# Hybrid encoder trunk on one core: down units in groups of four, a seventeenth weight tile, expert splits three ahead

## The chip, the cores and the metric

The kernel runs on one core of a Trainium2 chip. The metric is the device time of one execution in microseconds (us). Engines are named as the profile names them: PE (TensorE matmul), PEld (TensorE weight load), ACT (ScalarE), DVE (VectorE), POOL (GpSimd), SP (SyncE, which here issues the weight DMAs; SPq is its queue).

## The reference, cut to what matters

256 tokens of width 1024 go through two layers, all in float32. Layer 0 is a gated short convolution and a dense SwiGLU; layer 1 is differential attention and a mixture of eight experts. The part of this case is the mixture:

```
logits = t @ router                      # 256 tokens, 8 experts
top_v, top_i = top_k(logits, 2)          # two experts each, gates = softmax(top_v)
for e in range(8):
    out += combine[:, e] * ((silu(t @ w1[e]) * (t @ w3[e])) @ w2[e])
# w1[e], w3[e]: 1024 x 3584 ("up"); w2[e]: 3584 x 1024 ("down"); float32
```

The weights of the eight experts are 352.3 MB, and each of them is read once.

## The kernel before

**Units and tiles.** All weights pass through one `Stream` (L104 to L196). Its pieces are units of at most 128 x 2048 float32, which is 1 MB, or 8 KB of each partition. A unit is loaded by one DMA on SP (`load`, L142) into a *tile*, one of `SLOTS` = 16 buffers of 8 KB. The list `free` gives tiles out at its front and takes them back at its end.

**Wide and narrow experts.** The experts are ranked by their number of tokens; ranks 0 to 3 are *wide* (room for 128 tokens), ranks 4 to 7 *narrow* (64 tokens). `ORDER` makes them alternate: wide, narrow, wide, narrow and so on.
- A *wide unit* has to be split before use (`split_to`, L168): ACT writes the rounded upper part `whi` into a second tile (L180), DVE writes the rest `wlo` into a third one (L182), and the raw tile goes back to the list. PE then makes 12 matmuls of 512 columns with it (`proj`, L430): for each of two row blocks first the pass with `whi`, then the one with `wlo`, then again `whi` (two banks each). The two tiles go back once PE is done.
- A *narrow unit* is used as it is loaded (`proj_narrow`, L1138): 8 float32 matmul instructions, no split, one tile. Of the 32 up units of a narrow expert the last 16 are 768 KB (384 columns), all others are 1 MB.

**How far ahead.** After the matmuls of a unit, `release` (L192) gives its tiles back, splits the units up to `SPL` = 4 ahead of the one just used, and calls `fill`, which issues loads as long as there are free tiles and `spare` (L125) allows it. `spare` keeps back only what the splits of the next `AHEAD` = 8 releases need. ACT, DVE and PE each run in the order written. A new use of a tile waits for the end of the old one: a `whi` in a former raw tile waits for the DVE split that read it, a `whi` in a tile of a used unit waits for PE.

**Stages.** The mixture has nine stages (L1248). Stage e does the up units of the e-th expert and the down units of the one before it: 28 up units of a wide expert or 32 of a narrow one, and 14 down units. Stages 1, 3, 5 and 7 have narrow up units and wide down units, stages 2, 4 and 6 wide up and narrow down units; stage 0 has only up units (wide), stage 8 only down units (narrow). `merged` (L251) writes the order inside a stage: from the eighth up unit on, one down unit after each two up units, and what is left at the end.

**What else lies in a stage.** Counted in up units, `stage` (L1157) calls hooks: after the 3rd and the 6th the result of the expert before is scattered back to the tokens (`sct`, L1224 and L1225), after the 17th come the transposes of the route back, after the 22nd the tokens of the next expert are gathered (`tp`, L953 for a wide and L968 for a narrow one; the two parts of L953 lie one unit apart). When a chunk of hidden columns is done, ACT makes the SiLU (L1185), DVE multiplies (L1111, L1125), and four and five units later PE transposes the result (`tp`, L1105), which ACT and DVE then write back (L98, L99, L1130) into the `g3` tiles of 2 KB (`GT` = 16).

Of the kernel before, what the change touches and what calls it, by code (L numbers as in the profile page):

```python
# [36 lines left out]
LAMBDA_INIT = 0.8 - 0.6 * math.exp(-0.3 * 1)  # L37

UNIT = 2048
SLOTS = 16  # L40
SPL = 4
AHEAD = 8
GT = 16
GB = 3
HB = 1
NARROW = 64
# [23 lines left out]
def kernel(ctx: ExitStack, tc: tile.TileContext, x_in, positions, norm_mix, norm_ffn, conv_in,  # L70
                       conv_w, conv_out, attn_in, q_norm, k_norm, lam_q1, lam_k1, lam_q2, lam_k2, subln,
                       attn_out, ffn_w1, ffn_w3, ffn_w2, router, moe_w1, moe_w3, moe_w2, out):
    nc = tc.nc
# [30 lines left out]
    class Stream:  # L104
        def __init__(self, units, whole=0):
            self.units = units
            self.whole = whole
            self.free = list(range(SLOTS))
            self.raw = {}
            self.spl = {}  # L110
            self.nd = 0
            self.ns = 0
            self.done = 0

        def plain(self, i):
            return len(self.units[i]) == 4
# [8 lines left out]
        def spare(self):  # L125

            free, ns = len(self.free) - 1, self.ns
            for done in range(self.done, self.done + AHEAD):
                if free < 0:
                    return False  # L130
                while ns < min(done + SPL, len(self.units)):
                    if not self.plain(ns):
                        free -= 2
                        if free < 0:
                            return False
                        free += 1 if ns < self.nd else 0
                    ns += 1
                if done < len(self.units):
                    free += self.size(done)
            return True  # L140
# [51 lines left out]
        def release(self):  # L192
            self.free += self.spl.pop(self.done)[1]
            self.done += 1
            self.split_to(self.done - 1 + SPL)
            self.fill()  # L196

    def cols(w, c0, cw, k0, nk):
# [39 lines left out]
    WCH = [(0, 1024), (1024, 1024), (2048, 1024), (3072, 512)]  # L238
    NCH = [(0, 2048), (2048, 1536)]
    NDN = DFE * D // (P * UNIT)  # L240
    WAIT = 6

    def up_plan(narrow):

        for c0, cw in NCH if narrow else WCH:
            m = KD if narrow else KD * cw // UNIT
            for which in range(2):
                for j in range(m):
                    yield c0, cw, which, j, m

    def merged(up, down, narrow=False):  # L251

        d = 0
        for c, u in enumerate(up_plan(narrow) if up else ()):
            yield "up", u
            while down and d < (c + 1 - WAIT) // 2:
                yield "down", d
                d += 1
        for i in range(d, NDN if down else 0):
            yield "down", i  # L260

    def stage_units(up, w2, plain_up=False, plain_down=False):

        us = []
        for kind, u in merged(len(up) > 0, w2 is not None, plain_up):
            if kind == "up":
                c0, cw, which, j, m = u
                unit, plain = cols(up[which], c0, cw, j * KD // m, KD // m), plain_up
            else:
                unit, plain = pairs(w2, u), plain_down  # L270
            us.append((*unit, True) if plain else unit)
        return us
# [27 lines left out]
    st = Stream(units, n_static)  # L300
# [143 lines left out]
    def whole(xs, k0=0):  # L444
        return lambda k: (*xs, k0 + k)
# [62 lines left out]
    with ph1:  # L508
# [33 lines left out]
        for j in range(4):  # L542
            pc = cproj(3 * j)
            csb = work.tile([P, 512], F32, name="csb", tag="w0")
            S.activation(csb, pc, AF.Copy)
            spare(2)
            pv = cproj(3 * j + 1)
            u = work.tile([P, 2, NT], F32, name="u", tag="w1")
            V.tensor_tensor(u.rearrange("p m t -> p (m t)"), pv, csb, op=OP.mult)
            cv = work.tile([P, 2, NT], F32, name="cv", tag="w1")  # L550
            for m in range(2):
                wc = [cw_col[:, jj * 8 + 2 * j + m:jj * 8 + 2 * j + m + 1] for jj in range(3)]
                V.tensor_scalar(cv[:, m, :], u[:, m, :], wc[1], None, op0=OP.mult)
                for jj, o, i in ((0, slice(1, NT), slice(0, NT - 1)), (2, slice(0, NT - 1), slice(1, NT))):
                    V.scalar_tensor_tensor(cv[:, m, o], u[:, m, i], wc[jj], cv[:, m, o], op0=OP.mult, op1=OP.add)
            spare(2)
            pb = cproj(3 * j + 2)
            z = work.tile([P, 2, NT], F32, name="z", tag="w0")
            V.tensor_tensor(z, pb.rearrange("p (m t) -> p m t", m=2), cv, op=OP.mult)
            if j % 2 == 0:  # L560
                zt[j // 2] = gtile()
            c = slice(2 * (j % 2), 2 * (j % 2) + 2)
            split(zt[j // 2][0][:, c, :], zt[j // 2][1][:, c, :], z)
            spare(2)
# [76 lines left out]
    with ExitStack() as ph:  # L641
# [158 lines left out]
        down = Down(u0, 4, lambda k0: whole((oh, ol), k0))  # L800
# [97 lines left out]
    def one_hot(e, slots, scale=None, table=None):  # L898

        table = posm if table is None else table  # L900
        pe = p3.tile([P, NB, P], F32, name="pe", tag="pe", bufs=2)
        for b in range(NB):
            if scale:
                late["V"] = V.tensor_scalar(pe[:, b, :], slots, table[:, b, e:e + 1], scale[b], op0=OP.is_equal,
                                            op1=OP.mult)
            else:
                V.tensor_scalar(pe[:, b, :], slots, table[:, b, e:e + 1], None, op0=OP.is_equal)
        return pe
# [199 lines left out]
    def activate(h1, h3, n=0):  # L1108

        g = work.tile([P, 512], F32, name="g", tag="w1")  # L1110
        V.tensor_tensor(g, h3, h1, op=OP.mult)  # L1111
        parts = (p3.tile([P, 4, P], F32R, name="gh3", tag="g3", bufs=GT),
                 p3.tile([P, 4, P], F32R, name="gl3", tag="g3", bufs=GT))

# [7 lines left out]
    def activate_narrow(h1, h3, cw, n=0):  # L1122

        g = work.tile([P, 512], F32, name="g", tag="w1")
        V.tensor_tensor(g[:, :cw], h3, h1, op=OP.mult)  # L1125
        gn = p3.tile([P, 4, P], F32, name="gn3", tag="g3", bufs=GT)

# [29 lines left out]
    def stage(s, u0, xs, gt, hooks=(), bank_of=yd_bank):  # L1157
# [7 lines left out]
        yb = []  # L1165
        c = 0
        for u, (kind, v) in enumerate(merged(xs is not None, gt is not None, narrow), u0):
            if kind == "up":
                c0, cw, which, j, m = v
# [35 lines left out]
    class Back:  # L1205


        def __init__(self, pT, gate, narrow=False, final=False):
            self.pT, self.gate, self.narrow = pT, gate, narrow
            if final:  # L1210
                y = [p3.tile([P, 512], F32R, name=f"y{k}7", tag="g3", bufs=GT) for k in "hl"]
            else:
# [20 lines left out]
                V.tensor_tensor(x[:, b, c], bank, x[:, b, c], op=OP.add)  # L1233

    pe = one_hot(0, slot1, rstds)
    with tc.issue_after(late["S"].ins), tc.issue_after(late["V"].ins):
        st.release()
    xs = gather(pe)
# [8 lines left out]
    with tc.manual_schedule(engines={ET.PE, ET.Activation, ET.DVE}):  # L1247
        for e in range(NE + 1):  # L1248
# [31 lines left out]
            if e == NE:  # L1280
                end = Back(*backs.pop(NE - 1), not is_wide(NE - 1), final=True)
                end.scale(yb)
                for i in range(2):
                    c = slice(i * 512, (i + 1) * 512)
# [188 lines left out]
```

## Time and profile before

| | |
|---|---|
| median of three runs (1304.0, 1308.05, 1308.25) | 1308.05 us |
| profiled execution, its own time | 1304.43 us |
| its span, first to last instruction | 1302.6 us |
| PE busy | 1270.1 us (98%) |
| DVE busy, ACT busy | 754.9 us (58%), 608.6 us (47%) |
| DMA of the weights | 423.33 MB |

The profiled execution ends 1.8 us outside its span, and is 3.6 us shorter than the median. A busy PE is not PE at its peak, so the rows below are read by what a group of matmuls takes from one start to the next. A row of the chain (the work that ended last, followed back from the end) is: start us, duration us, engine, output tile, line, and the number of instructions merged. [...]

### The profile page before, as it was taken

The page shows a single profiled execution, that of the slowest core. Times are in us where ns is not written, and L with a number is a line of the kernel's source. Part 1 is how long each engine was busy: PE and PEld are TensorE (multiplying, and loading weights), DVE is VectorE, ACT ScalarE, POOL GpSimd, SP SyncE. Part 2 cuts the span into 40 slices and gives each one's busy share as a digit, 9 for nine tenths or more (in the row PEclk, how much of TensorE's full clock was granted, in tenths as well). Part 3 has the DMA queues.
Part 4 walks back from the last instruction along what each step waited for, and adds up shares of the span by engine and source line. Part 5 has one row for each costly group of instructions (what it writes and reads, how often), then busy time and mean ns, then how long its engine had stood idle before and what let it go on. Part 6 is the DMA issues. An engine that isn't in the chain of part 4 may idle for free.

```text
span 1302.6 us, 16445 instructions
## 1 busy us (share of the span) xinstructions
PE 1270.1 (98%) x6275; PEld 885.1 (68%) x6275; DVE 754.9 (58%) x995; ACT 608.6 (47%) x674; POOL 2.9 (0%) x12
## 2 busy tenths in 40 slices
PE   6999999999999899999999999999999999999997
PEld 6998888888767788556767546676635676754552
DVE  7976555547776698243865334586524387543340
ACT  5535444436676685234654233565423365523330
POOL 0000000000000000000000000000000000000000
PEclk9999999999999899999999999999999999999998
DMA  7964655546430499999999999999999999999995
GB/s 254 393 207 141 244 176 193 192 129 227 177 130 30 154 345 333 413 425 423 397 423 416 387 426 425 414 399 420 388 425 425 424 393 418 420 389 426 425 426 229
DMA packets 109652, 426.02 MB, mean 327 GB/s; under 512 B 9053, under 2 KB 23422, under 8 KB 87166
## 3 DMA queue, kind: packets, MB, share of 16 engines
q1 hardware_dynamic: 109134, 423.33, 82.6%
q0 software_dynamic: 432, 1.57, 0.3%
q8 instruction: 51, 0.84, 0.2%
q14 instruction: 35, 0.29, 0.1%
HBM read 423.82 MB, written 1.05 MB: 326 GB/s over the span
## 4 chain that ended last, share of the span: by engine, by line
PE 91%; DVE 4%; ACT 2%; DMA 2%; issue 0%; SPq 0%; DVEq 0%; ACTq 0%
PE h L441 33%; PE h L1146 14%; PE y L441 11%; PE y L1146 8%; PE yd L441 8%; PE qkv L441 4%; DVE wlo L182 2%; PE mm L535 2%; PE mm L536 2%; PE mm L534 2%; PE tp L1105 2%; PE tp L953 1%; ACT whi L180 1%; DMA raw<-in_moe_w_dram 1%; PE tp L968 1%; PE tp L421 1%
## 5 line engine op out<-in xcount | busy, mean ns | idle before, releaser
L182 DVE TENSOR_TENSOR wlo<-raw,whi 128x2048 fp32r<-128x2048 f32 (+1 forms) x298 | 536.2, 1823 | 349.9 <-ACT whi L180 302.0
L180 ACT ACTIVATE whi<-raw 128x2048 fp32r<-128x2048 f32 (+1 forms) x298 | 450.9, 1538 | 429.2 <-PE h L441 160.8
L1146 PE MATMUL h<-raw,xn 128*64 128x512 f32 (+1 forms) x1024 | 206.2, 545 | 0.0
L441 PE MATMUL h<-whi,xh 128*128 128x512 f32 x448 | 148.6, 401 | 0.0
L1146 PEld LDWEIGHTS h<-raw,xn 128*64 128x64 f32 x1024 | 68.2, 136 | 117.8 <-issue 111.9
L441 PE MATMUL h<-wlo,xh 128*128 128x512 f32 x448 | 144.3, 392 | 2.3 <-DVE wlo L182 2.3
L441 PE MATMUL h<-whi,xl 128*128 128x512 f32 x448 | 143.7, 390 | 0.0
L1146 PE MATMUL y<-raw,gn 128*64 128x512 f32 x448 | 105.2, 601 | 0.0
L441 PEld LDWEIGHTS h<-whi,xh 128*128 128x128 f32 x448 | 81.2, 189 | 31.5 <-ACT whi L180 9.7
L441 PEld LDWEIGHTS h<-wlo,xh 128*128 128x128 f32 x448 | 83.7, 188 | 21.7 <-DVE wlo L182 4.1
L441 PEld LDWEIGHTS h<-whi,xl 128*128 128x128 f32 x448 | 84.1, 188 | 18.3
L441 PE MATMUL y<-whi,gh 128*128 128x512 f32 x224 | 75.0, 416 | 0.0
L441 PE MATMUL h<-wlo,hh 128*128 128x512 f32 (+1 forms) x192 | 71.9, 375 | 0.0
L441 PE MATMUL h<-whi,hh 128*128 128x512 f32 (+1 forms) x192 | 71.8, 374 | 0.0
L441 PE MATMUL h<-whi,hl 128*128 128x512 f32 (+1 forms) x192 | 71.5, 372 | 0.0
L441 PE MATMUL y<-wlo,gh 128*128 128x512 f32 x224 | 69.4, 391 | 0.0
L441 PE MATMUL y<-whi,gl 128*128 128x512 f32 x224 | 69.2, 390 | 0.0
L1146 PEld LDWEIGHTS y<-raw,gn 128*64 128x64 f32 x448 | 28.5, 136 | 50.9 <-issue 45.6
L441 PEld LDWEIGHTS y<-whi,gh 128*128 128x128 f32 x224 | 38.1, 188 | 30.8 <-issue 22.6
L535 PE MATMUL mm<-hl,whi 128*128 128x256 f32 x192 | 55.0, 287 | 0.1
L534 PE MATMUL mm<-hh,whi 128*128 128x256 f32 x192 | 55.0, 287 | 0.0
L536 PE MATMUL mm<-hh,wlo 128*128 128x256 f32 x192 | 54.8, 286 | 0.0
(262 smaller groups left out, 1417.2 us busy)
## 6 DMA issues: line engine op xcount, KB each, us to landing
raw<-in_moe_w_dram SPq DMA_DIRECT2D x287, 1024.0 KB, 12.2
raw<-in_moe_w_dram SPq DMA_DIRECT2D x64, 768.0 KB, 14.8
raw<-in_ffn_w_dram SPq DMA_DIRECT2D x33, 1024.0 KB, 5.0
raw<-in_conv_in_dram SPq DMA_DIRECT2D x12, 1024.0 KB, 9.5
raw<-in_attn_in_dram SPq DMA_DIRECT2D x12, 1024.0 KB, 5.1
raw<-in_conv_out_dram SPq DMA_DIRECT2D x4, 1024.0 KB, 13.8
raw<-in_attn_out_dram SPq DMA_DIRECT2D x4, 1024.0 KB, 5.0
x<-in_x_dram SPq DMA_DIRECT2D x2, 512.0 KB, 4.5
```

The costliest lines, as they stand in the source:

```text
L180: S.activation(hi[:, c], r[:, c], AF.Copy)
L182: V.tensor_tensor(lo[:, c], r[:, c], hi[:, c].bitcast(F32), op=OP.subtract)
L421: T.transpose(tp[:, c * P:(c + 1) * P], src[:, (c0 + c) * P:(c0 + c + 1) * P], ident)
L441: T.matmul(o, lhsT=l, rhs=m[:, kk, c0 + i * cw:c0 + (i + 1) * cw], start=first and kk + j == 0, stop=last and kk == nk - 1 and j == len(pa ...
L534: T.matmul(o, lhsT=w, rhs=hh[:, k, :], start=k == 0, stop=False)
L535: T.matmul(o, lhsT=w, rhs=hl[:, k, :], start=False, stop=False)
L536: T.matmul(o, lhsT=lo[:, k, m * P:(m + 1) * P], rhs=hh[:, k, :], start=False, stop=k == KD - 1)
L953: T.matmul(tp[:, c * P:(c + 1) * P], lhsT=hm[b][:, k * P:(k + 1) * P], rhs=pe[:, b, :], start=b == 0, stop=b == NB - 1)
L968: T.matmul(tp[:, k * NARROW:(k + 1) * NARROW], lhsT=hm[b][:, k * P:(k + 1) * P], rhs=pe[:, b, :NARROW], start=b == 0, stop=b == NB - 1)
L1105: T.transpose(tp[:, c * P:(c + 1) * P], gv[:, c // 2, c % 2, :], ident)
L1146: T.matmul(bank[halves(t), :n], lhsT=xt(kk), rhs=w[:, kk, c0:c0 + n], start=first and kk == 0, stop=last and kk == nk - 1)
```

## The change

[...] `merged` puts down units in groups of four behind each eighth up unit, so a stage with 28 up units has groups after the 8th, 16th and 24th and two down units at its end; one with 32 has three groups and the last two down units after the 32nd. From the last attention units on, splits are made three units ahead of the one just used, where it was four; the transposes of L1105 stay at four and five units.

```diff
-SLOTS = 16
+SLOTS = 17
 SPL = 4
 AHEAD = 8
-GT = 16
+GT = 15
@@ class Stream
+            self.ahead = SPL
@@ def spare(self):
-                while ns < min(done + SPL, len(self.units)):
+                while ns < min(done + self.ahead, len(self.units)):
@@ def release(self):
-            self.split_to(self.done - 1 + SPL)
+            self.split_to(self.done - 1 + self.ahead)
@@
-    WAIT = 6
@@ def merged(up, down, narrow=False):
             yield "up", u
-            while down and d < (c + 1 - WAIT) // 2:
-                yield "down", d
+            if down and (c + 1) % 8 == 0:
+                for d in range(d, min(d + 4, NDN)):
+                    yield "down", d
                 d += 1
@@ before the first expert
     pe = one_hot(0, slot1, rstds)
+    st.ahead = SPL - 1
@@ def kernel(**inputs):
-    nc = _bacc.Bacc("TRN2", target_bir_lowering=False, num_devices=1, dynamic_dma_scratch_size=4096)
+    nc = _bacc.Bacc("TRN2", target_bir_lowering=False, num_devices=1, dynamic_dma_scratch_size=2048)
```

## Rows read from the trace of the kernel before

**Rows 1.** The page: shares of the chain by engine.
```profile
PE 91%; DVE 4%; ACT 2%; DMA 2%; issue 0%; SPq 0%; DVEq 0%; ACTq 0%
```
**Rows 2.** Table by stretch: stages 3, 4, both, 5 with 6, 7, 8, and 0.
```profile
741.27:839.04 97.77, 97.77 (x479) 53.60 (x475) 40.35 (x27) 33.89 (x25) 0.00 (x0) 1.00 1.01 424
839.04:955.15 116.11, 115.34 (x531) 79.60 (x531) 75.15 (x53) 61.05 (x47) 0.00 (x0) 1.00 1.00 403
741.27:955.15 213.88, 213.11 (x1009) 133.20 (x1006) 115.50 (x79) 94.94 (x72) 0.00 (x0) 1.00 1.01 413
955.15:1169.11 213.96, 213.22 (x1009) 133.20 (x1006) 115.50 (x79) 94.94 (x72) 0.00 (x0) 1.00 1.01 413
1169.11:1263.49 94.38, 94.38 (x448) 49.76 (x446) 37.62 (x24) 30.96 (x23) 0.00 (x0) 1.00 1.01 426
1263.49:1291.70 28.21, 28.16 (x127) 9.74 (x126) 1.41 (x2) 2.07 (x5) 0.00 (x0) 1.00 0.77 324
442.62:528.04 85.42, 83.96 (x402) 69.92 (x403) 69.04 (x87) 59.25 (x46) 0.00 (x0) 1.00 0.92 336
```
**Rows 3.** The chain in stage 3: narrow up units (h), wide down units (y).
```profile
741.27 5.15 PE h L1146 x24
...
747.09 5.30 PE h L1146 x24
...
753.06 3.58 PE h L1146 x16
756.64 2.94 PE y L441 x12
...
793.18 2.73 PE h L1146 x16
...
801.59 1.98 PE tp L953 x16
```
**Rows 4.** The chain in stages 4 and 8: wide up units (h), narrow down units (y).
```profile
850.16 8.16 PE h L441 x36
...
872.26 0.47 PE tp L1105 x4
...
874.59 0.68 PE tp L1105 x4
...
880.72 1.87 PE y L1146 x8
882.59 5.71 PE h L441 x24
...
1277.77 13.91 PE y L1146 x64
```
**Rows 5.** The chain where stage 3 ends and stage 4 begins.
```profile
827.87 2.96 PE y L441 x12
...
830.85 1.92 ACT whi L180
...
832.79 2.30 DVE wlo L182
...
835.11 1.93 ACT whi L180
...
841.34 2.30 DVE wlo L182
...
843.69 2.57 PE h L441 x10
```
**Rows 6.** Timeline of PE at the same place; in brackets the idle time before.
```profile
843.69 0.73 PE L441 MATMUL h<-wlo,xh 128*128 128x512 f32 x2 [0.77 <-DVE wlo L182]
```
**Rows 7.** Table by stretch, inside stage 0 (DVE is the third engine).
```profile
480.00:500.00 20.00, 19.47 (x91) 15.90 (x89) 19.66 (x28) 14.20 (x11) 0.00 (x0) 1.00 0.97 338
```
**Rows 8.** Groups of instructions from 440 us on (busy us, mean ns | idle before): ACT.
```profile
L1185 ACT ACTIVATE s<-h 128x512 f32<-128x512 f32 (+1 forms) x44 | 23.7, 576 | 38.9 <-PE h L1146 29.8 <-PE h L441 8.5
...
L98 ACT ACTIVATE gh<-tp 128x512 fp32r<-128x512 f32 x28 | 16.4, 587 | 48.9 <-PE tp L1105 48.9
```

## The prediction

> **What bounds the kernel now.** I read the page first. PE is busy 98% of the span (table above), and the chain that ended last lies 91% on PE [rows 1]. Busy is no proof of pace, so next I read the table by stretch for the stages of the mixture. Stages 1 and 2, 3 and 4, 5 and 6 are three like pairs; the two measured ones last 213.88 and 213.96 us, with PE idle for 0.77 us in each [rows 2]. The DMA is close behind: a pair loads two experts, 84 units of 1.0486 MB or 88.1 MB, and at the 426 GB/s of stage 7 [rows 2] that takes 207 us. So PE is the bound by 7 us per pair, and the DMA is what stands next. Inside a pair they change places: stage 3 takes 97.8 us for a load of 103.4, stage 4 takes 116.1 [rows 2]; the tiles loaded ahead carry the difference. Then I read the chain, where each change from narrow to wide matmuls and back shows as a small surcharge [rows 3, 4], and the one place in a pair where PE waits for a split [rows 5, 6].
>
> **Part 1: fewer changes between narrow and wide.** Narrow up units run at 5.15 us for three (x24), but at 5.30 or 3.58 (x24, x16) behind full-width matmuls [rows 3]: 0.15 more. A wide unit takes 8.16/3 = 2.72 [rows 4], but 2.94 behind a narrow one [rows 3]: 0.22 more. One excursion costs 0.37. Stage 3 now has 13 (14 down units, the last two together), and afterwards four. But the gather lies between narrow and wide today and will stand inside a narrow run, which makes two excursions of its two parts: six. It saves 7 x 0.37 = 2.6 us in stages 1, 3 and 5. Stage 7 has no gather: 9 x 0.37 = 3.3, with its route back about 3.5.
> In stage 4 a lone narrow down unit takes 1.87 where eight take 13.91, 1.74 each: 0.13 more. The next two wide units take 5.71 for 5.44: 0.27 more; if a transpose lies between, it pays 0.21 instead (0.68 for 0.47) [rows 4]. Ten lone units make 3.8 us. Afterwards there are three groups, but the transposes of the chunk just finished come after the third and the fourth down unit, so each group is two excursions, six times 0.34 = 2.0 us. It saves 1.7, I keep 1.7.
> Sum: 3 x (2.6 + 1.7) + 3.5 = **16.4 us less**, all of it on PE, which is the path. No matmul is added or removed.
>
> **Part 2: what the splits wait for.** Nothing in ACT's or DVE's work changes in amount; its start does. I walked the list of free tiles through both versions by the code. Since the loads take every tile that `spare` leaves, a split finds only the tiles that came back last.
> Before, in the alternation, `whi` waits for the unit five before and `wlo` for the one four before. Only where a run of wide units begins, at the end of stage 3, do two splits in a row find a raw tile that the split before has just given back. Then ACT and DVE can't overlap. The chain shows it: the first `whi` starts at 830.85, when the wide unit four before has ended (827.87 + 2.96), `wlo` follows at 832.79, the next `whi` not before 835.11, and the third `wlo` ends at 843.64; PE takes it up at 843.69 [rows 5] after an idle 0.77 [rows 6]. Three splits in series took 12.87 us from release to use. Counting what PE did meanwhile (two narrow units 2.73, three wide ones 2.94 + 2.72 + 2.72, a transpose 0.47, the `whi` pass 0.46) gives 12.04, so a stall of 0.83; the trace has 0.77.
> After, splits start one unit later, and the list gives this pattern at every step from narrow to wide: the first `whi` waits for the fourth unit before, the second and the third each for the raw tile of the split before, from the fourth on a split waits for the unit three before. So the 12.87 us start when the fourth narrow unit before the run has ended, and until the third wide unit asks for its `wlo` PE has only three narrow units, two wide ones and a pass to do: 2.94 + 2.72 + 0.46 = 6.12 plus the narrow ones. The stall at each place:
> Stages 1, 3, 5: behind up unit 8, narrow 5.15 and a scatter 0.67 + 0.15 (from 752.39 to 753.06, and its surcharge) [rows 3]: 12.09, stall 0.8. Behind 16: 11.27, stall 1.6. Behind 24: the gather's two parts of about 2 us [rows 3] lie in between, no stall. Behind 32: the 768 KB units are 1.29 each ((2.73 - 0.15)/2) [rows 3], 9.99, stall 2.9, and this one takes the place of the 0.77 of today. Together 5.3.
> Stages 2, 4, 6: three narrow units 5.22 + 0.13, two transposes 1.36, wide 5.90: 12.6, stall 0.3; then DVE, which has two halves of the transposed result to write besides, keeps the next two splits late by about as much again. 0.7 a group, three groups: 2.1.
> Stage 7: 0.8 + 1.6, behind 24 without a gather 2.9, behind 32 only two wide units follow, two splits in series, 1.3. Together 6.6.
> Stage 0: DVE is already busy 19.66 of 20 us there [rows 7], and PE idle 1.46 in the stage [rows 2]. Starting a wide split one unit later takes 2.72 of its cover: steady, a split needs 4.25 and has 2 x 2.72 + 0.46 = 5.9, a margin of 1.65, less the SiLU or the product of a chunk. I take 1.5 us, with 0 and 4 as ends.
> Sum: 3 x (5.3 + 2.1 - 0.8) + 6.6 + 1.5 = **27.9 us more**.
>
> **Part 3: loads.** The seventeenth tile and one split fewer held let loads run 1.5 units further ahead (14.2 to 15.7 units issued beyond the one in use in stage 3, 13.4 to 14.9 in stage 4, by the same walk). With PE at 216 us a pair the DMA, at 207, has slack, so this is worth nothing while PE is later; narrow runs of eight (13.7 us, against 19.7 of load) draw on less than three units of the lead. `GT` 15: the two or four tiles that a chunk takes were freed by down units already behind it in the new order; the scratch is for the few loads of gains by POOL, which fall before the mixture. Both nothing, covered by that order; a late gain would cost at most its own transfer, a few us, once.
>
> The total is -16.4 + 27.9 = +11.5 us on the profiled execution: 1304.4 + 11.5 = 1315.9. The median of the runs shown lies 3.6 above that execution; I go up by about a third of it: **1317 us**.
>
> **Rivals.** (a) *The seventeenth tile ends the bubble.* For: PE's idle 0.77 does repeat with each pair, and it ends when a split gets its tile [rows 5, 6]. Against: `spare` lets the loads have the tile. Then the new order costs nothing, the old bubbles go as well (3 x 0.77), and the time is 1304.4 - 16.4 - 2.3 = 1285.7; on the scale of the median some 1287. [...]
> (b) *PE gains, the DMA takes part of it back.* If the series of splits is milder than I think, a pair falls to 209.6, but with stage 3 at 95.2 us against 103.4 of load the lead falls by 8 us of load, 3.3 units, and is refilled only in stage 4. A dry spell of 2 us per pair and 2 in stage 7 would leave 16.4 + 2.3 - 8 = 10.7 gain, 1294; with the median's offset 1295.
> (c) *The margin of 1.65 us doesn't hold inside long wide runs.* Every run of eight also carries scatters, SiLUs, products and transposes; where two of them meet, a split comes later than the three units allow. It decides once they take more than 1.65 us of ACT or DVE in one unit (two SiLUs of 0.58 and a rewrite of 0.59 [rows 8] just do). With 1.5 us in each of the 12 runs (three per stage 0, 2, 4, 6) that is 18 more: 1335, on the slow side of the forecast.
> That the order isn't as said can be left aside: it is plain from the generator, and 14 down units come out in each stage.
>
> **How the numbers follow.** Forecast (splits in series cost more than the saved surcharges) 0.60, spread 1305 to 1328 by the ends of stage 0 and by stalls 30% smaller or larger (27.9 x 0.3 = 8). Rival (a) 0.14, (b) 0.11, (c) 0.15. The range 1289 to 1334 leaves out most of (a) and the upper part of (c). A measurement of this kernel can tell about 0.3%, 3.9 us, from no change. Faster: (a), (b) and a little of the forecast, 0.27. Same: the lower end of the forecast, 0.15. Slower: the rest, 0.58.
>
> **What would show it.** In the profile after: PE waits on `wlo` (L182) summing to some 28 us instead of 2.3, lying on the second and third wide unit of each run, with chains of `whi` and `wlo` in turn at 4.27 us per unit; narrow pieces of up to x64 instructions where x16 stood; stage 3 with its matmuls 2.6 us shorter; DMA mean below 413 GB/s in a pair. If the waits on `wlo` are under 10 us in all, (a) or (b) is right, and waits on the loads tell (b). If they are above 40 and lie inside the runs, it is (c).

## The result and the profile after

The changed kernel takes 1338.6 us (median of four) against 1308.1: **2.6% slower**, ratio 1.0258 with a 95% interval of 1.023 to 1.0287. The forecast was slower by 9 us; it is slower by 30. The profiled execution lasts 1338.70 us with a span of 1336.9, 34.3 more than before.

The page after, with busy time of the engines and the chain's shares by engine:

```profile
PE 1270.9 (95%) x6275; PEld 894.4 (67%) x6275; DVE 753.7 (56%) x995; ACT 607.1 (45%) x674; POOL 2.9 (0%) x12
...
PE 70%; DVE 13%; ACT 9%; DMA 6%; issue 1%; SPq 0%; ACTq 0%; DVEq 0%
```

The work is the same and the busy times with it; what is new is idle time of PE, and a chain that now lies 22% on DVE and ACT where it was 6% [rows 1]. By stretch: stages 1 and 2, 3 and 4 together, then stages 3, 4, 7 and 0. The columns, in [rows 2] too, are the stretch, its length, busy us (and instructions) of PE, PEld, DVE, ACT and POOL, the granted clock as a share of full speed, the DMA share, and GB/s.

```profile
530.54:753.13 222.59, 212.38 (x1000) 136.02 (x1002) 113.36 (x77) 94.23 (x72) 0.00 (x0) 0.98 0.97 391
753.13:975.43 222.30, 212.64 (x1009) 135.52 (x1006) 115.07 (x79) 94.33 (x72) 0.00 (x0) 0.99 0.98 397
...
753.13:853.76 100.63, 97.25 (x483) 54.99 (x479) 40.10 (x30) 34.65 (x27) 0.00 (x0) 1.00 1.00 414
853.76:975.27 121.51, 115.23 (x526) 80.39 (x526) 74.97 (x50) 59.68 (x46) 0.00 (x0) 0.99 0.96 383
1197.74:1297.48 99.74, 93.88 (x453) 51.10 (x450) 38.04 (x25) 31.26 (x24) 0.00 (x0) 1.00 1.00 417
444.29:530.54 86.25, 85.11 (x402) 69.53 (x403) 69.14 (x87) 61.28 (x47) 0.00 (x0) 1.00 0.89 321
```

Against [rows 2] a pair has grown by 8.4 us (222.3 for 213.9; the first pair by 9.4), in all 26; stage 7 by 5.4, stage 0 by 0.8. That leaves 2 of the 34.3 us, nearly all of it ahead of the mixture: its first wide matmul starts at 444.1 us, and before at 442.4. Traces of kernels that are the same up to there differ by as much as 6.0 us at this point (448.4 in the run with the order alone), so this part is not put down to the change. The DMA moves 397 GB/s in a pair, less than the 413 before [rows 2]; whether the loads bind is tested below. Next, what PE waited for (us in total, times, longest):

```profile
PE y L442 <- DVE wlo L183: 16.2, 14, 1.3
PE tp L1086 <- DVE gl L99: 12.5, 3, 4.2
...
PE h L442 <- DVE wlo L183: 7.5, 11, 1.3
```

Lines after L111 stand one or two lower than before. The waits on `wlo` are 23.7 us; they were 2.3. The second row is new, and nothing in the forecast stands for it. Last, a step from narrow to wide in the chain of stage 5, behind the 16th up unit (start, duration, what):

```profile
1003.84 8.76 PE h L1147 x40
1012.62 1.92 ACT whi L181
1014.56 2.30 DVE wlo L183
1016.89 1.93 ACT whi L181
...
1023.12 2.30 DVE wlo L183
...
1025.46 2.59 PE y L442 x10
```

`whi` and `wlo` alternate and never overlap: 12.84 us from the first start to the use, the same figure as at the one place before where it happened [rows 5]. Timeline of PE: every wait in stages 3 and 4 of after (idle time in brackets).

```profile
776.26 0.73 PE L442 MATMUL y<-wlo,gh 128*128 128x512 f32 x2 [0.77 <-DVE wlo L183]
803.16 0.73 PE L442 MATMUL y<-wlo,gh 128*128 128x512 f32 x2 [1.26 <-DVE wlo L183]
851.37 0.73 PE L442 MATMUL y<-wlo,gh 128*128 128x512 f32 x2 [1.28 <-DVE wlo L183]
855.64 0.73 PE L442 MATMUL h<-wlo,xh 128*128 128x512 f32 x2 [1.26 <-DVE wlo L183]
894.58 0.73 PE L442 MATMUL h<-wlo,xh 128*128 128x512 f32 x2 [0.31 <-DVE wlo L183]
926.37 0.41 PE L1086 MATMUL tp<-ident,pe 128*128 128x128 f32 x2 [4.17 <-DVE gl L99]
966.28 0.50 PE L442 MATMUL h<-wlo,xh 128*128 128x512 f32 x1 [0.53 <-DVE wlo L183]
```

They lie behind up units 8, 16 and 32 of stage 3 and behind 8, 16 and 24 of stage 4; behind 24 of stage 3, where the gather stands, there is none. Each idle time is some 0.15 us short of the true gap, since the last matmul before a wait is drawn longer (0.61 us) than the next one would have let it be (0.46). The 4.17 us belong to the route back, which comes after the 17th up unit: one wide unit behind the group of four. Its transpose needs one of two `tp` banks, both hold chunk transposes from that group, and their rewrite on DVE (`gl`) stands behind the third split of the series. DVE at that moment:

```profile
923.33 2.29 DVE L183 TENSOR_TENSOR wlo<-raw,whi 128x2048 fp32r<-128x2048 f32 x1 [1.98 <-ACT whi L181]
925.54 0.68 DVE L99 TENSOR_TENSOR gl<-tp,gh 128x512 fp32r<-128x512 f32 x1
```

And behind the 4.17 us PE runs on slowly. By stretch, the idle time, the time after, and the next (granted clock is the third column from the end):

```profile
922.20:926.37 4.17, 0.00 (x1) 0.03 (x1) 3.04 (x3) 3.87 (x4) 0.00 (x0) 1.00 0.99 412
926.37:929.90 3.53, 3.53 (x13) 2.96 (x14) 3.04 (x4) 0.00 (x0) 0.00 (x0) 0.59 1.05 404
929.90:933.00 3.10, 3.10 (x13) 2.48 (x13) 0.00 (x0) 1.39 (x1) 0.00 (x0) 0.91 1.04 403
```

### The profile page after: what moved, and what is told of

The parts are those of the page before. It is cut to its first block, busy times and chain, and to the rows that moved or that the text cites. A ratio compares the mean times of both kernels' runs of the same rounds, so it can differ in the third digit from the quotient of the medians.

```text
span 1336.9 us, 16379 instructions
## 1 busy us (share of the span) xinstructions
PE 1270.9 (95%) x6275; PEld 894.4 (67%) x6275; DVE 753.7 (56%) x995; ACT 607.1 (45%) x674; POOL 2.9 (0%) x12
## 4 chain that ended last, share of the span: by engine, by line
PE 70%; DVE 13%; ACT 9%; DMA 6%; issue 1%; SPq 0%; ACTq 0%; DVEq 0%
PE h L442 26%; DVE wlo L183 10%; PE h L1147 10%; ACT whi L181 8%; PE yd L442 8%; PE y L442 6%; DMA raw<-in_moe_w_dram 6%; PE qkv L442 4%; PE y L1147 3%; PE mm L536 2%; PE mm L537 2%; PE mm L535 2%; PE tp L954 1%; PE tp L969 1%; PE tp L422 1%
## 5 line engine op out<-in xcount | busy, mean ns | idle before, releaser
L1147 PE MATMUL h<-raw,xn 128*64 128x512 f32 (+1 forms) x1024 | 200.2, 542 | 0.0
L442 PE MATMUL h<-wlo,xh 128*128 128x512 f32 x448 | 147.3, 399 | 7.5 <-DVE wlo L183 7.5
L442 PEld LDWEIGHTS h<-wlo,xh 128*128 128x128 f32 x448 | 84.1, 191 | 31.8 <-DVE wlo L183 15.1
L1147 PE MATMUL y<-raw,gn 128*64 128x512 f32 x448 | 101.9, 598 | 0.0
L442 PE MATMUL y<-whi,gh 128*128 128x512 f32 x224 | 71.4, 400 | 0.0
L442 PEld LDWEIGHTS y<-wlo,gh 128*128 128x128 f32 x224 | 40.2, 188 | 33.0 <-DVE wlo L183 25.8
```

The source lines that it names most:

```text
L442: T.matmul(o, lhsT=l, rhs=m[:, kk, c0 + i * cw:c0 + (i + 1) * cw], start=first and kk + j == 0, stop=last and kk == nk - 1 and j == len(pa ...
L1147: T.matmul(bank[halves(t), :n], lhsT=xt(kk), rhs=w[:, kk, c0:c0 + n], start=first and kk == 0, stop=last and kk == nk - 1)
```

## The experiments

Theory A: the new order makes the splits of the first three wide units of a run go in series, because the tile for `whi` is the raw tile of the split before; the stalls on `wlo` and the route back's wait both come from that. Theory B: splitting three ahead is the cost. Theory C: the loads are. The chain of after speaks for C at first sight, with stretches of 14 us on `raw` loads (6% of the span).

### Order alone, and four ahead again

```diff
# e1_order_alone: the kernel before, with the new order of down units
-            while down and d < (c + 1 - WAIT) // 2:
-                yield "down", d
+            if down and (c + 1) % 8 == 0:
+                for d in range(d, min(d + 4, NDN)):
+                    yield "down", d
# e2_four_ahead: the changed kernel
-    st.ahead = SPL - 1
```

> The kernel before with the new order of down units alone (16 tiles, GT 16, splits four ahead). Theory A (runs of narrow units make the splits of the next wide units go in series, and the route back of a wide stage waits behind them): as slow as the changed kernel, 1335 to 1345 us; the first four splits of a run in series, the wait of the route back's transpose longer than 4.2 us (about 6.5), since one more split stands ahead of the rewrite it waits for. Theory B (splitting three ahead is what costs): no slower than before, 1290 to 1310. Theory C (late loads): slower than the changed kernel, as loads run 1.5 units less ahead.

> The changed kernel with splits four ahead again (17 tiles, new order). Theory A: 1335 to 1345 us, within 0.5% of the changed kernel: stalls behind narrow up units a little smaller (4.6 instead of 5.2 per stage), the route back's wait larger (6.5 instead of 4.2). Theory B: back to 1290 to 1310. Theory C: about 1338.

Measured: 1344.3 us, ratio 1.0295 (1.0273 to 1.0317), and 1342.8 us, ratio 1.03 (1.0282 to 1.0317). Both are as slow as A said, and B falls as the only cause: the order alone is enough. C, which also had the first one slower than the changed kernel, is left to the runs below. The tile makes no visible difference between the two. The third split does move waits: against the changed kernel those of the second on `wlo` fall from 23.7 us to 13.4, more than was expected, but the route back waits longer, as expected, since the fourth split goes in series too and stands ahead of the rewrite, and a wait for a bank of the scatter comes in. In sum a pair takes 225.0 us there and 222.3 in the changed kernel. PE's waits in the second run:

```profile
PE tp L1086 <- DVE gl L99: 19.6, 3, 6.6
...
PE y L442 <- DVE wlo L183: 6.8, 7, 1.3
PE h L442 <- DVE wlo L183: 6.6, 9, 1.3
PE y L442 <- DVE x L1234: 4.8, 3, 1.6
```

### The route back three units later

```diff
# e3_route_later
-{1: early, 3: lambda: back(0), 6: lambda: back(1), 17: hot, 22: ahead}
+{1: early, 3: lambda: back(0), 6: lambda: back(1), 20: hot, 22: ahead}
# e5_route_wide_only
-{1: early, 3: lambda: back(0), 6: lambda: back(1), 17: hot, 22: ahead}
+{1: early, 3: lambda: back(0), 6: lambda: back(1), 20 if e in (2, 4, 6) else 17: hot, 22: ahead}
```

> The changed kernel with the route back's hook after the 20th up unit, not the 17th. Theory A: the 4.17 us wait in stages 2, 4 and 6 goes, and with it the stretch at half clock behind it (1.7 us): 3 x 5.9 = 17.6 less, about 1321 us; the waits on wlo stay (some 24 us). If the waits only move to the next group: 1334 to 1340. Theory C: unchanged, 1338.

Measured: 1335.0 us, ratio 1.0232 (1.0215 to 1.0249). A misses the total by 14 us, but by stretch the stages that it spoke of fell as it said. Stages 0 and 4 of this run:

```profile
441.00:544.25 103.25, 94.15 (x411) 76.77 (x409) 69.94 (x88) 61.43 (x47) 0.00 (x0) 0.92 0.76 272
...
861.25:977.39 116.14, 113.80 (x525) 79.17 (x525) 74.82 (x50) 59.46 (x46) 0.00 (x0) 1.00 0.99 400
```

Stage 4 fell from 121.5 to 116.1, and 2 and 6 as well; stage 0 rose by 15.9, from its first wide matmul on (the expectation below has 13). There the later hook waits 5.3 us for `gl`, the gather behind it 2.3 us for a copy on DVE, and the clock over the whole stage is 0.92. So the hook was moved in stages 2, 4 and 6 alone:

> The changed kernel with the route back's hook after the 20th up unit in stages 2, 4 and 6 alone; in the other stages it stays after the 17th. In the run that moved it everywhere, stages 2, 4 and 6 fell from 121.5 to 116.2 us, but stage 0 got 13 us longer. Theory A (the route back waits behind splits in series): 3 x 5.3 = 16 less than the changed kernel, 1322 us. Theory C (loads are the bound that stays): above 1333.

Measured: 1319.4 us, ratio 1.0103 (1.0066 to 1.0139). By stretch stages 2, 4 and 6 fell by 6.3, 5.3 and 5.3 us, so some 17 of the 30 are the route back's wait with the slow stretch behind it; of the other 2, nearly all lies ahead of the mixture, where the two kernels are the same. Stages 3 and 4 of this run together:

```profile
744.10:961.10 217.00, 211.25 (x1008) 134.24 (x1006) 114.98 (x79) 94.14 (x72) 0.00 (x0) 1.00 1.00 407
```

The waits on `wlo` are nearly as before this edit:

```profile
PE y L442 <- DVE wlo L183: 16.1, 14, 1.3
...
PE h L442 <- DVE wlo L183: 8.1, 13, 1.3
```

### whi and wlo trade tiles

```diff
# e4_swap_tiles
-                    hi, a = self.slot("whi", F32R)
                     lo, b = self.slot("wlo", F32R)
+                    hi, a = self.slot("whi", F32R)
```

> The changed kernel, but a split takes the first free tile for wlo and the second for whi. Then the raw tile just given back is awaited by DVE, which freed it itself, and whi of the next unit needs only the end of a used unit, so ACT and DVE overlap again. Theory A: nearly all waits on wlo go (24 to about 5 us) and the route back's with them; the saved surcharges remain: 1296 to 1306 us, a little faster than before. Theory B and C: hardly changed, 1330 to 1340.

Measured: 1311.5 us, ratio 1.0053 (1.0036 to 1.007). One exchanged line takes 27 us off the changed kernel, though the loads and the three ahead are as they were: C falls with it, and B as the main cause. It lies 5 us above the expected range, for two waits that A had let go and that stayed in part:

```profile
PE y L442 <- DVE wlo L183: 6.7, 10, 1.1
...
PE tp L1086 <- DVE gl L99: 6.4, 3, 2.4
```

With the later route back as well, as `20 if e in (2, 4, 6) else 17: hot`:

> The changed kernel with traded tiles for whi and wlo and the route back after the 20th up unit in stages 2, 4 and 6, splits still three ahead. Theory A: the run with traded tiles alone gave 1311.5; its 2.4 us wait of the route back and the slow clock behind it go, 3 x 4 = 12: 1299 us. The rest to the run with all three changes is what three ahead costs once ACT and DVE overlap (5 to 10 us). If the route back only moves the wait: 1308 to 1312.

Measured: 1298.3 us, ratio 0.9935 (0.9914 to 0.9956). The total is as expected, in part by luck: stages 2, 4 and 6 fell by 2.2, 4.2 and 2.3 us, 8.7 where 12 stood, since in 2 and 6 the wait had been 2.0 us, in 2 with a granted clock of 1.00 in the 1.6 us behind it (last section). The other 4 lie ahead of the mixture, which this edit does not touch.

### All three causes taken away

The new order and 17 tiles stay:

```diff
# e6_all_three: the changed kernel
-17: hot
+20 if e in (2, 4, 6) else 17: hot
-                    hi, a = self.slot("whi", F32R)
                     lo, b = self.slot("wlo", F32R)
+                    hi, a = self.slot("whi", F32R)
-    st.ahead = SPL - 1
```

> New order and 17 tiles, with all three causes taken away: whi and wlo trade tiles (no series), splits four ahead, route back after the 20th up unit in stages 2, 4 and 6. Theory A: a pair of stages falls from 222.3 to about 209 us, the saved surcharges alone remaining: 1286 to 1294 us. Theory C: the loads (207 us a pair) hold it at 1296 or more.

Measured: 1290.7 us, ratio 0.9899 (0.9863 to 0.9934), 1% faster than the kernel before. The step from three ahead to four is worth 7.6 us here, within the 5 to 10 of the expectation before. Stages 3 and 4 of this run:

```profile
735.17:833.20 98.03, 96.54 (x484) 55.44 (x481) 41.49 (x29) 37.22 (x29) 0.00 (x0) 1.00 1.01 419
833.20:945.50 112.30, 112.30 (x526) 79.72 (x525) 73.65 (x51) 56.07 (x44) 0.00 (x0) 1.00 1.02 420
```

The same with the old lines of `merged` tells what the order is worth:

> The run with all three causes taken away, but in the old order (17 tiles, splits four ahead, tiles traded). What it lacks against that run is the new order alone. Theory A: no saved surcharges (16 to 18 us for three pairs and stage 7), so 1300 to 1306 us, as before; the seventeenth tile by itself brings nothing. If the gain of that run came from the tile: 1290.

Measured: 1302.7 us, ratio 0.9991 (0.9968 to 1.0014). Its stages 3 and 4, with PE never idle:

```profile
739.95:837.93 97.98, 97.98 (x480) 53.74 (x477) 42.77 (x30) 37.80 (x28) 0.00 (x0) 1.00 1.02 424
837.93:952.62 114.69, 114.69 (x530) 79.81 (x530) 73.10 (x50) 57.61 (x45) 0.00 (x0) 1.00 1.00 405
```

212.7 us a pair against 210.3, and of these 1.6 are a wait for a bank that only the new order has (below). So the order saves 3.9 us a pair in matmuls; the forecast had 4.3. Over stages 1 to 7, first in the new order, then in the old:

```profile
528.27:1249.63 721.36, 716.91 (x3462) 456.74 (x3461) 382.02 (x260) 310.18 (x240) 0.00 (x0) 1.00 1.01 420
528.09:1259.77 731.68, 731.68 (x3461) 450.59 (x3461) 384.35 (x260) 317.58 (x240) 0.00 (x0) 1.00 1.01 417
```

That is 10.3 us, and 15.1 without the three waits of 1.6, where part 1 of the forecast had 16.4.

### The old order with splits three ahead

```diff
# e7_old_order: the changed kernel with the old order
+            while down and d < (c + 1 - 6) // 2:
+                yield "down", d
```

> The changed kernel with the old order of down units (17 tiles, splits three ahead). By the walk of the tile list each wide unit of stage 3 waits for the wide unit three before: behind two narrow units of 768 KB a stall of 0.9 us, seven times, and at the end of the stage three splits in series with 4 us of stall. Theory A: some 9 us a pair and 6 in stage 7, 1330 to 1340 us, so three ahead costs by itself in the old order too. If only the order is at fault: 1300 to 1308.

Measured: 1352.2 us, ratio 1.0349 (1.0311 to 1.0386): slower still. Three ahead costs in the old order too, so B names a second cause. The two do not add up: the order alone is 3.0% slower, this 3.5%, both together 2.6%. The time is 12 us above the expected range: stage 3 takes 106.7 us as expected (+9), but stage 4 takes 118.9 and stage 7 105.6, where I had 116 and 100. In stage 4 the transposes of a chunk wait 2.15 us for a copy on DVE, which the expectation did not have. The chain in stage 3, at one of seven lone wide units: PE waits for its split, and that for the wide unit three before.

```profile
825.81 2.96 PE y L441 x12
...
828.80 1.92 ACT whi L181
...
830.74 2.30 DVE wlo L183
...
833.09 2.58 PE y L441 x10
```

### Traded tiles in the kernel before, sixteen tiles, earlier scatters

The exchanged line of `e4_swap_tiles` in the kernel before:

> The kernel before with whi and wlo trading tiles alone. Theory A: the one wait on wlo per pair (0.77 us idle, 0.9 in all) goes, nothing else: 3 x 0.9 = 2.8 less, within 0.3% of before. If series of splits cost more than PE's idle time shows: 1290 to 1298.

Measured: 1301.5 us, ratio 0.9973 (0.9953 to 0.9993). The series cost the old order some 3 us, as its idle time shows [rows 6]: each pair falls by 1.1. "Nothing else" did not hold: stage 0 takes 87.8 us for 85.6, with a wait of 2.0 us for a copy on DVE (1.5 before) and matmuls that take 0.85 us a pair behind it, where 0.46 is usual, and the start of the mixture comes 2.7 us earlier; why was not tried.

```diff
# e11_sixteen: all three causes taken away, and
-SLOTS = 17
+SLOTS = 16
-GT = 15
+GT = 16
# e12_scatter_early: all three causes taken away, and
-3: lambda: back(0), 6: lambda: back(1)
+2: lambda: back(0), 4: lambda: back(1)
```

> The run with all three causes taken away, with 16 tiles (and GT 16). A pair takes 210.3 us there, its loads 207, so the seventeenth tile should hardly matter: 1289 to 1294 us. If the loads were close to binding, one unit less ahead would cost 2.5 us a pair and more: 1297 to 1305.

Measured: 1290.9 us, ratio 0.9884 (0.9859 to 0.9909), the same as with 17. The seventeenth tile brings nothing, and with it C is out: at 210 us a pair one unit less of lead isn't felt.

> The run with all three causes taken away, and the two scatters after the 2nd and the 4th up unit, not the 3rd and the 6th. In that run the first wide down unit of stages 3, 5 and 7 waits 2.2 us for a bank that the second scatter's add on DVE gives back behind two wlo. Theory A: 3 x 2.2 = 6.6 less, 1284 us; the floor by the loads (3 pairs of 207 instead of 210.3) would stop it at about 1281. If the add only waits elsewhere: 1288 to 1293.

Measured: 1291.0 us, ratio 0.9877 (0.9853 to 0.9901): no gain, the second branch. The wait was 1.4 us idle, 1.6 in all, and not 2.2. Stage 3 fell by 1.8 us and stage 4 rose by 2.0. The wait moved from the wide down unit to the scatter of the next stage, which now comes before its input is ready. PE's waits in the run before this edit, then in this one:

```profile
PE y L442 <- DVE x L1234: 4.3, 3, 1.4
```

```profile
PE sct L1225 <- DVE yl L1220: 4.5, 3, 1.5
```

## Why the prediction was right or wrong, step by step

**The sign, and the mechanism of part 2, were right.** The walk of the tile list gave series of three splits at each step from narrow to wide, and the traded tiles showed that they are the cause. The sizes on `wlo` also held. Forecast for stages 1, 3 and 5: 0.8, 1.6, none, 2.9; idle times in stage 3 plus 0.15 each: 0.92, 1.41, none, 2.84 (the last in two halves). For stage 7 6.6; measured five waits of 5.8 idle in all, so about 6.5. Together the waits on `wlo` are 23.7 us of idle time where "some 28" stood, with the 0.15 each 27.5.

**Part 1 was right in size.** 4.3 us a pair were forecast and 3.9 found, between the two runs without stalls on splits; in all 15.1 of 16.4. In the changed kernel itself only about 3 a pair are found when the idle times are taken off with 0.15 each, since a wait costs more than that. The wide units behind up unit 16 of stage 3, first in the changed kernel, then with all three causes taken away:

```profile
795.35:805.59 10.24, 8.91 (x39) 6.72 (x38) 8.27 (x7) 4.88 (x3) 0.00 (x0) 1.00 1.02 427
778.30:786.60 8.30, 8.30 (x39) 6.88 (x38) 7.66 (x7) 2.29 (x2) 0.00 (x0) 1.00 1.01 420
```

That is 1.9 us for an idle 1.26: two matmuls behind a wait take 0.57 us to the next start where 0.46 is usual, and some short gaps are not marked as waits. Summed in this way over the waits on `wlo` in stages 3 and 4, against runs without them, the series costs a pair 7.8 us and not 6.3, so the saving of part 1 is there in full (about 4.5 us).

**The step that failed** is the sum for stages 2, 4 and 6: "0.7 a group, three groups: 2.1". I counted what the series does to the wide units that use it, and stopped there. On ACT and DVE the rewrites of the chunk transposes stand behind the third split; they hold both `tp` banks; and the hook after the 17th up unit asks for a bank one unit after the group. The forecast even names the two transposes and counts their length, but not who needs their banks next. That is 4.3 us of wait a pair (4.17 + 0.15). Then comes a term that wasn't in the sum at all: PE at a lower clock behind the wait, an estimate of 1.7 us (3.5 us at 0.59 of full speed, some 1.45 lost, and 0.3 in the stretch after). Without both a pair would be 222.3 - 6.0 = 216.3 where the forecast had 216.2; the run with the later hook in those stages has 217.0. It took 6.3, 5.3 and 5.3 us off them, so this step is some 17 of the 21.6 us by which the forecast of 1317 was off. Most of the rest is stage 7, 5.4 us longer where 6.6 - 3.5 = 3.1 was forecast, and the start of the mixture.

**Stage 0** took 0.8 us more for a forecast of 1.5.

**The rivals.** (a), the seventeenth tile ends the bubble, is refuted: with 16 tiles the repaired kernel is as fast, and with 17 the bubble came 25 times. The bubble is a wait for a tile, but the number of tiles was not the lack: which of two free tiles was given to which engine decided (1338.6 us, and 1311.5 with the two exchanged). (b), the DMA takes part of the gain back, is out by the same run. (c) came near the measured time (1335) for a reason that did not hold: in stages 1 to 7 of the changed kernel no wait on `wlo` lies beyond the third unit of a run. It was the right side for the wrong cause.

## What to carry to other kernels

When tiles are taken from a list in turn, ask for each new tile which engine freed it last: a tile that the second engine of a chain has just freed should go to that engine, not to the first one, or the two stop overlapping, as here, where three splits took 12.84 us in series and the exchange took 27 us off. When a queue gets late work, follow not only who uses that work but everything queued behind it, down to the banks that it holds and the next one to ask for them (here a wait of 4.17 us in stage 4). The bunched order saved nearly all of its surcharges here, 15.1 us of 16.4, but the kernel became faster only after both had been put right (0.9935 of the time before, and 0.9899 with splits four ahead again, where the change alone gave 1.0258).

## What the runs showed of the hardware

PE's granted clock fell with the longest waits of these runs, and stayed low into the work behind them. The 0.59 over the 3.5 us behind the idle 4.17 us is a mean: 1.00 for the first 0.66 us, then 0.50 to 930.44 us. By stretch:

```profile
926.37:927.03 0.66, 0.66 (x7) 0.66 (x7) 0.66 (x1) 0.00 (x0) 0.00 (x0) 1.00 1.05 413
927.03:930.44 3.41, 3.41 (x9) 2.71 (x10) 2.38 (x4) 0.00 (x0) 0.00 (x0) 0.50 1.05 403
930.44:933.00 2.56, 2.56 (x12) 2.06 (x11) 0.00 (x0) 1.39 (x1) 0.00 (x0) 1.00 1.04 402
```

In the run with four ahead the wait is 6.55 us, with a granted clock of 0.66 over it, so if it fell from 1.00 to 0.50 in one step there too, it was at 0.50 from about 923 us on (an estimate from that mean); the wait, and what came behind it:

```profile
920.96:927.51 6.55, 0.00 (x1) 0.03 (x1) 4.58 (x4) 4.68 (x4) 0.00 (x0) 0.66 1.00 424
927.51:931.50 3.99, 3.99 (x13) 3.41 (x14) 3.04 (x4) 0.00 (x0) 0.00 (x0) 0.50 1.00 404
```

Around 2 us the length of the wait did not decide it alone. Behind waits of 2.02 and 2.37 us (traded tiles, stages 2 and 4), of 2.15 us (old order, three ahead, stage 4) and of 2.03 us (all three causes taken away, stage 0; 1.0 us behind the end of the wait, from 500.66 us on, a pair of matmuls takes 0.86 us where 0.46 is usual):

```profile
696.90:698.50 1.60, 1.60 (x10) 1.47 (x11) 1.60 (x1) 0.00 (x0) 0.00 (x0) 1.00 0.99 420
911.36:914.50 3.14, 3.14 (x12) 2.66 (x13) 3.14 (x4) 0.00 (x0) 0.00 (x0) 0.58 0.99 410
930.58:934.00 3.42, 3.42 (x17) 2.94 (x18) 0.45 (x1) 0.00 (x0) 0.00 (x0) 1.00 1.02 400
501.00:503.00 2.00, 2.00 (x6) 1.52 (x5) 2.00 (x2) 0.00 (x0) 0.00 (x0) 0.50 1.01 381
```

What makes the difference was not tried. Stages 3 and 7 of after, with waits of 1.3 us and less, have a granted clock of 1.00 over all of their 100.6 and 99.7 us.
